# Order of the seven products, of the early operand splits and of the residual additions in the FFN down projection of a hybrid decoder layer

## The chip, the cores and the metric

The kernel runs on one core of one Trainium2 chip. The metric is the device time of one execution in microseconds, and the median of several executions is compared. The engines of a core are TensorE (PE, the matrix products), VectorE (DVE), ScalarE (ACT), GpSimd (POOL) and SyncE (SP, which here only issues DMAs). Each engine works through its own list of instructions in the order in which they were put there.

## The reference

One layer of a decoder for 1024 prompt tokens and 8 sample tokens (one new token for each of 8 sequences), width 1024, all in float32. The change lies in the last part, the feed-forward block:

```python
gate = h2 @ lp['w_ffn_gate']                    # (tokens, 2816)
up = h2 @ lp['w_ffn_up']                        # (tokens, 2816)
...
gc = _causal_dwconv(gate_ext, lp['ffn_conv_w'], L) + lp['ffn_conv_b']
x = x + gt2 * ((jax.nn.silu(gc) * up) @ lp['w_ffn_down'])
...
y_prompt = _rmsnorm(xp, final_norm_w)
```

Before it stand the input projection, a gated delta rule, a sliding-window attention and an output projection, which the change does not touch.

## The kernel before

**Precision.** A float32 operand is split into a high part (ACT, line 127, a copy into a rounded format) and a low part (DVE, line 128, the operand minus its high part). The helper `mm3` (lines 176 to 180) makes each product of two operands from three matmuls: high by high (L178), high by low (L179), low by high (L180).

**Seven products instead of eight.** The gate, up and down projections use a Strassen-Winograd scheme: both operands are cut into 2 x 2 blocks, and seven products of sums of blocks, numbered 1 to 7 in the down projection, replace eight products of blocks. Their results are added with signs to the four blocks of the output.

**Gate and up (`ffn_gate_up`, `pair_product`).** A loop goes over pairs `f` of 128-wide column blocks of the 2816, eleven pairs. For each pair the gate products are made, then the convolution and the activation on DVE and ACT (`conv`), then the up products. Both token halves `p` = 0 and 1 go through the seven products; `keep` copies an intermediate sum out of PSUM with ACT (L1563), and `up` evacuates a block with DVE (L1638 adds a kept copy, L1640 multiplies by the activated gate). When the four blocks of a token half are ready, `act_operands` has POOL make five sums of blocks (L1655), and writes these (L1658, one DMA from POOL's queue) and two plain blocks (L1657, from SP's queue) to `xd` in DRAM. `xd[i, g]` is the moving operand of kind `i` for the pair `g` = 0 to 10: kinds 0 to 4 are POOL's sums, 5 and 6 are plain blocks.

**Down (`ffn_down`).** A step is one product number `i` and one pair `g`; there are 7 x 11 = 77 steps, in the order of `chains`. `made[i]` says which kind of `xd` a product reads and which weight blocks: one block, or two, with their sum or difference. `fetch(s)` loads step `s`: the weight block (L1687), the second block if there is one (L1690) with the sum or difference on POOL (L1691), and the moving operand (L1692), all loads from SP's queue, into one of five raw buffers; then `split` writes the high and low parts into one of 13 rooms (`tags`), so that at most 13 steps are fetched ahead of PE. The rooms are those of the operands of the gate and up projections, and come free as the last up products have read them.

A step on PE has 24 matmuls: 4 column blocks `j` x 2 token halves `p` in eight PSUM banks, three matmuls each, summed over the eleven `g` of a product. Two products of one chain follow each other in the same banks without being cleared, so that the second adds to the first. After the last `g` of a product, `take` adds each bank to the residual `x1` (L1407, and L1411 with L1412 for the sample tokens): for products with one place in the output (4, 7, 6) directly from PSUM, for those with two places after an ACT copy (L1714) into one of eight buffers `copies`. All additions of a bank are issued at once, before the next product's matmuls:

```python
def take(ps, i, p, j):
    if len(home[i]) > 1:
        ...
        nc.scalar.copy(r, ps)
        ps = r
    for d, q, sign in home[i]:
        self.add_gated(2 * p + q, ps, j + 4 * d, 40, ...)
```

The last product, 6, is not in this loop: it runs bank by bank, with the final norm (`norm_rows`) of the rows that are ready between its banks.

**Order.** The functions issue instructions with priorities in the order of the program; a scheduler fixes each engine's list when the program is made, by times that it assumes. `tc.issue_after(x)` places the instructions of its block that run on the engine of `x` behind `x` in that list; it adds no wait at run time. So the splits of the first steps stand in DVE's and ACT's lists among the evacuations of the last up products, and the matmuls of the first steps fill PE between those products.

Of the kernel before, what the change touches and what calls it, by code (L numbers as in the profile page):

```python
# [22 lines left out]
KC = 8  # L23
# [39 lines left out]
class Step:  # L63
# [1479 lines left out]
    def pair_product(self, psum, w, pairs, evac, after={}):  # L1543

        nc = self.nc
        bank = lambda pl, tag, n: self.t(pl, [P, 512], tag, bufs=2)[:, :n]
        width = [QUARTERS[2 * p][1] for p in range(2)]
        x, v, y, r = {}, {}, {}, {}  # L1550

        def product(ps, p, i, first=True):

            (wh, wl), (xh, xl) = w[i], self.X[p][i]
            kw = {} if first else {"skip_group_check": True}
            with self.tc.issue_after(after[i].ins) if i in after else nullcontext():
                for k in range(4):
                    self.mm3(ps, wh[:, k, :], wl[:, k, :], xh[:, k, :], xl[:, k, :], first and k == 0, k == 3, **kw)

        def keep(p, i):  # L1560
            self.turn = (self.turn + 1) % KC
            r[p, i] = self.copies[:, self.turn, :width[p]]
            nc.scalar.copy(r[p, i], x[p])  # L1563

        for p in pairs:
            x[p] = bank(self.pmm, "mm", width[p])
            product(x[p], p, 0)
            keep(p, 0)
        for p in pairs:
            y[p] = bank(psum, "wy", width[p])  # L1570
            product(y[p], p, 1)
            evac(p, 0, 0, y[p], r[p, 0])
        for p in pairs:
            product(x[p], p, 2, False)
            keep(p, 1)
        for p in pairs:
            v[p] = bank(psum, "wv", width[p])
            product(v[p], p, 3)
        for p in pairs:
            product(x[p], p, 4, False)  # L1580
            keep(p, 2)
            evac(p, 1, 1, v[p], r[p, 2])
        for p in pairs:
            product(x[p], p, 5, False)
            evac(p, 1, 0, x[p], None)
        for p in pairs:
            product(v[p], p, 6, False)
            evac(p, 0, 1, v[p], r[p, 1])

    def ffn_gate_up(self, pool, pool2, psum, f, w, first):  # L1590

        nc, I = self.nc, self.I
        fcw = self.fcw
        z = [self.t(pool, [P, NT + 2], "fz", bufs=2) for _ in range(2)]
        for i in range(2):
            nc.gpsimd.memset(z[i][:, 0:2], 0.0)
        a = [self.act_tile(pool2) for _ in range(2)]
        done = {}

        def gate(p, i, q, ps, r):  # L1600
            lo, n = QUARTERS[2 * p + q]
            zq = z[i][:, 2 + lo:2 + lo + n]
            if r is None:
                nc.scalar.copy(zq, ps)
            else:
                nc.vector.tensor_tensor(zq, ps, r, op=ALU.add)
            done[p, i] = done.get((p, i), 0) + 1
            if done[p, i] == 2:
                conv(p, i)

        def conv(p, i):
            c, n = HALF[p]
            e = min(c + n, NP)
            zi, ai = z[i], a[i]
            col = lambda j: fcw[:, j, f + i:f + i + 1]
            nc.vector.tensor_scalar(ai[:, c:e], zi[:, 2 + c:2 + e], col(2), col(3), op0=ALU.mult, op1=ALU.add)
            for j in (0, 1):
                nc.vector.scalar_tensor_tensor(ai[:, c:e], zi[:, j + c:j + e], col(j), ai[:, c:e],  # L1618
                                               op0=ALU.mult, op1=ALU.add)
            if p:  # L1620
                nc.gpsimd.tensor_copy(self.fzl[:, f + i, :], zi[:, NP:NP + 10])
                nc.vector.scalar_tensor_tensor(ai[:, NP:], zi[:, 2 + NP:], col(2), self.fsp[:, f + i, :],
                                               op0=ALU.mult, op1=ALU.add)
            th = zi[:, c:c + n]
            nc.scalar.activation(th, ai[:, c:c + n], AF.Tanh)
            nc.vector.scalar_tensor_tensor(ai[:, c:c + n], th, 1.0, ai[:, c:c + n], op0=ALU.add, op1=ALU.mult)

        if first:
            ss, r = self.norm_at
            self.pair_product(psum, w, (0,), gate, {2: ss, 4: r})  # L1630
        self.pair_product(psum, w, (1,) if first else (0, 1), gate)
        w = self.pair_weights(pool, I["w_ffn_up"][0], f, nc.vector if first else None)

        def up(p, i, q, ps, r):
            lo, n = QUARTERS[2 * p + q]
            aq = a[i][:, lo:lo + n]
            if r is not None:
                nc.vector.tensor_tensor(r, ps, r, op=ALU.add)  # L1638
                ps = r
            nc.vector.tensor_tensor(aq, aq, ps, op=ALU.mult)  # L1640
            done[p, i] += 1
            if done[p, 0] == done[p, 1] == 4:
                self.act_operands(p, f // 2, a)

        self.pair_product(psum, w, (0, 1), up)
# [17 lines left out]
    def ffn_down(self, pool, psum):  # L1663
# [4 lines left out]
        made = {5: (2, (1, 1)), 3: (5, (0, 1), (1, 1), ALU.subtract), 4: (6, (1, 0), (0, 0), ALU.subtract),  # L1668
                7: (4, (1, 0), (1, 1), ALU.add), 1: (0, (0, 0), (1, 1), ALU.add), 2: (1, (0, 0)),
                6: (3, (0, 0), (0, 1), ALU.add)}  # L1670
        chains = ((4, 7), (3, 5), (1,), (2,), (6,))
        home = {3: ((0, 0, 1), (1, 1, 1)), 5: ((1, 0, 1), (0, 0, -1)), 4: ((0, 1, 1),), 7: ((0, 0, 1),),
                1: ((0, 0, 1), (1, 1, 1)), 2: ((0, 1, 1), (1, 1, -1)), 6: ((1, 1, 1),)}
        steps = [(i, g) for c in chains for i in c for g in range(G)]
        ready = {}
        less = []

        def fetch(s):
            i, g = steps[s]
            if s % 5 == 3:  # L1680
                ready["raw"] = self.t(self.bm, [P, KC, QW], "bmh0").rearrange("p k n -> p (k n)")
            raw = self.t(self.pw, [P, n + 512], "raw", bufs=3) if s % 5 < 3 else \
                ready["raw"][:, (s % 5 - 3) * 1040:(s % 5 - 3) * 1040 + n + 512]
            at, *src = made[i]
            src = [x if type(x) is not tuple else
                   I["w_ffn_down"][0][(2 * g + x[0]) * P:(2 * g + x[0] + 1) * P, 512 * x[1]:512 * x[1] + 512] for x in src]
            nc.sync.dma_start(raw[:, n:], src[0])  # L1687
            if len(src) > 1:
                other = self.t(self.pw, [P, 512], "ws", bufs=3)
                nc.sync.dma_start(other, src[1])  # L1690
                nc.gpsimd.tensor_tensor(raw[:, n:], raw[:, n:], other, op=src[2])  # L1691
            nc.sync.dma_start(raw[:, :n], self.xd[at, g])  # L1692
            room = self.room(tags[s % len(tags)], [P, KC * QW])
            hi, lo = room[:, :n + 512], room[:, n + 512:2 * (n + 512)]
            self.split(hi, lo, raw)
            ready[s] = hi, lo
            if s == 5:
                less.append(self.t(pool, [P, KC, 9], "less"))
                nc.gpsimd.tensor_scalar(less[0], self.mT[:, 40:48, :], -1.0, None, op0=ALU.mult)
                for j in (2, 3, 4):  # L1700
                    self.x1[j] = self.t(pool, [P, NT], f"x1_{j}")
                for j in range(2, 8):
                    nc.gpsimd.dma_start(self.x1[j], self.x1d[j])

        def step(s, ps, p, j, first, last, kw):
            hi, lo = ready[s]
            x, w = slice(256 * p, 256 * p + 256 + 4 * p), slice(n + j * P, n + j * P + P)
            self.mm3(ps, hi[:, w], lo[:, w], hi[:, x], lo[:, x], first, last, **kw)

        def take(ps, i, p, j):  # L1710
            if len(home[i]) > 1:
                self.turn = (self.turn + 1) % KC
                r = self.copies[:, self.turn, :256 + 4 * p]
                nc.scalar.copy(r, ps)  # L1714
                ps = r
            for d, q, sign in home[i]:
                self.add_gated(2 * p + q, ps, j + 4 * d, 40, self.mT[:, 40:48, :] if sign > 0 else less[0])

        banks = [(self.pmm, "mm", 2), (psum, "wv", 2), (psum, "wy", 2)] * 2 + [(self.pmf, "mm", 1), (psum, "nr", 1)]
        order = [(p, j) for j in range(4) for p in range(2)]  # L1720
# [1 line left out]
        for c in chains[:-1]:  # L1722
            ps = {(p, j): self.t(pl, [P, 512], tag, bufs=k)[:, :256 + 4 * p] for (p, j), (pl, tag, k) in zip(order, banks)}
            for i in c:
                for g in range(G):
                    while done < min(s + len(tags), len(steps)):
                        fetch(done)
                        done += 1
                    for p, j in order:
                        step(s, ps[p, j], p, j, g == 0 and i == c[0], g == G - 1, {"skip_group_check": True} if i != c[0] else {})  # L1730
                        if g == G - 1:
                            take(ps[p, j], i, p, j)
                    s += 1
        while done < len(steps):
            fetch(done)
            done += 1
# [3 lines left out]
        for k, (p, j) in enumerate((p, j) for p in (1, 0) for j in range(4)):  # L1740
            ps = self.t(self.pmf if k % 3 == 2 else self.pmm, [P, 512], "mm", bufs=1 if k % 3 == 2 else 2)[:, :256 + 4 * p]
            for g in range(G):
                step(s + g, ps, p, j, g == 0, g == G - 1, {})
            take(ps, 6, p, j)
            for c in chunks[k]:
                for _ in self.norm_rows(pool, psum, [c]):
                    pass
# [229 lines left out]
```

## Time and profile before

| | |
|---|---|
| time, median of 3 runs | 2173.14 us (2170.6 to 2176.24) |
| the profiled execution, its own time | 2178.02 us |
| its span from the first to the last instruction | 2176.3 us |
| mean granted TensorE clock | 0.974 |
| PE busy | 2084.8 us (96%) |
| DVE busy | 1394.8 us (64%) |
| ACT busy | 845.2 us (39%) |
| POOL busy | 517.6 us (24%) |

The times in the profile are microseconds from the start of the span. L1407 is line 1407 of the kernel. The last gate and up products run from about 1880, the down projection takes over between 1914 and 1939, and the last product runs from about 2123 on. A matmul stands with the time from its start to its modelled end, and starts about 0.12 us after the one before; a PE that is shown as idle had no matmul in that time at all. An entry such as `[2.00 <-ACT bml L1714]` says that the engine stood idle for 2.00 us before this instruction and which engine and line ended it.

### The profile page before, as it was taken

The page shows a single profiled execution, that of the slowest core. Times are in us where ns is not written, and L with a number is a line of the kernel's source. Part 1 is how long each engine was busy: PE and PEld are TensorE (multiplying, and loading weights), DVE is VectorE, ACT ScalarE, POOL GpSimd, SP SyncE. Part 2 cuts the span into 40 slices and gives each one's busy share as a digit, 9 for nine tenths or more (in the row PEclk, how much of TensorE's full clock was granted, in tenths as well). Part 3 has the DMA queues.
Part 4 walks back from the last instruction along what each step waited for, and adds up shares of the span by engine and source line. Part 5 has one row for each costly group of instructions (what it writes and reads, how often), then busy time and mean ns, then how long its engine had stood idle before and what let it go on. Part 6 is the DMA issues. An engine that isn't in the chain of part 4 may idle for free. (4 is left out here: it accounts for less than half of the span.)

```text
span 2176.3 us, 41336 instructions
## 1 busy us (share of the span) xinstructions
PE 2084.8 (96%) x16309; PEld 1960.8 (90%) x16309; DVE 1394.8 (64%) x2773; ACT 845.2 (39%) x2102; POOL 517.6 (24%) x589
## 2 busy tenths in 40 slices
PE   7998999999899999999999999999999999999998
PEld 4985887899898988998999999898999999989998
DVE  4656667374555756665323665478888788796885
ACT  4655445334234244344322032244343343333542
POOL 1000000021221110111110300003646556574330
PEclk8999998899999999999999999899999999999999
DMA  8256442151332321221317763511333332389862
GB/s 279 80 137 206 147 138 79 40 143 41 84 82 57 77 56 41 62 66 51 89 60 227 222 188 105 173 62 59 111 102 93 108 98 88 130 270 332 273 200 81
DMA packets 298980, 268.68 MB, mean 123 GB/s; under 512 B 60558, under 2 KB 246321, under 8 KB 298770
## 3 DMA queue, kind: packets, MB, share of 16 engines
q1 hardware_dynamic: 293586, 247.22, 37.5%
q0 software_dynamic: 4912, 18.29, 2.3%
q8 instruction: 128, 2.10, 0.4%
q14 instruction: 66, 0.54, 0.1%
q10 hardware_dynamic: 288, 0.52, 0.1%
HBM read 207.29 MB, written 61.07 MB: 123 GB/s over the span
## 5 line engine op out<-in xcount | busy, mean ns | idle before, releaser
L178 PE MATMUL mm<-b1h,wh 128*128 128x384 f32 (+1 forms) x1392 | 458.0, 330 | 4.5 <-ACT z L764 2.1
L180 PE MATMUL mm<-b1h,wl 128*128 128x384 f32 (+1 forms) x1392 | 453.0, 326 | 3.8 <-DVE wl L128 3.8
L179 PE MATMUL mm<-b1l,wh 128*128 128x384 f32 (+1 forms) x1392 | 450.6, 324 | 0.3 <-DVE b1l L128 0.3
L178 PEld LDWEIGHTS mm<-b1h,wh 128*128 128x128 f32 x1392 | 264.1, 190 | 14.8 <-issue 4.7
L180 PEld LDWEIGHTS mm<-b1h,wl 128*128 128x128 f32 x1392 | 263.9, 190 | 10.3 <-issue 5.5
L179 PEld LDWEIGHTS mm<-b1l,wh 128*128 128x128 f32 x1392 | 264.5, 190 | 3.6 <-issue 1.9
L127 ACT ACTIVATE wh<-raw 128x1024 fp32r<-128x1024 f32 x75 | 78.6, 1048 | 154.5 <-PE mm L179 77.6
L128 DVE TENSOR_TENSOR wl<-raw,wh 128x1024 fp32r<-128x1024 f32 x74 | 92.0, 1243 | 63.9 <-ACT wh L127 63.2
L178 PE MATMUL mm<-pk,w 128*128 128x260 f32 (+1 forms) x440 | 125.1, 285 | 3.0 <-ACT bml L1563 2.4
L179 PE MATMUL mm<-pk,w 128*128 128x260 f32 (+1 forms) x440 | 124.9, 284 | 0.8 <-DVE pk L128 0.8
L180 PE MATMUL mm<-pk,w 128*128 128x260 f32 (+1 forms) x440 | 124.7, 284 | 0.0
L178 PE MATMUL mm<-b2h,wh 128*128 128x384 f32 (+1 forms) x384 | 123.2, 322 | 0.4 <-ACT wh L127 0.4
L180 PE MATMUL mm<-b2h,wl 128*128 128x384 f32 (+1 forms) x384 | 122.0, 320 | 1.3 <-DVE wl L128 1.3
L179 PE MATMUL mm<-b2l,wh 128*128 128x384 f32 (+1 forms) x384 | 122.7, 320 | 0.0
L128 DVE TENSOR_TENSOR w<-ws,w 128x512 fp32r<-128x512 f32 x88 | 74.6, 849 | 36.5 <-ACT w L127 36.5
L178 PE MATMUL mm<-bmh,w 128*128 128x260 f32 (+1 forms) x320 | 92.0, 287 | 0.8 <-DVE fa L1640 0.7
L180 PE MATMUL mm<-bmh,w 128*128 128x260 f32 (+1 forms) x320 | 91.8, 287 | 0.0
L1563 ACT COPY bml<-mm 128x256 f32<-128x256 f32 (+1 forms) x132 | 49.1, 373 | 104.1 <-PE mm L180 97.6
L178 PEld LDWEIGHTS mm<-pk,w 128*128 128x128 f32 x440 | 83.3, 189 | 3.8 <-ACT bml L1563 3.0
L179 PEld LDWEIGHTS mm<-pk,w 128*128 128x128 f32 x440 | 83.4, 190 | 1.0 <-DVE pk L128 1.0
L180 PEld LDWEIGHTS mm<-pk,w 128*128 128x128 f32 x440 | 83.6, 190 | 0.0
L1618 DVE SCALAR_TENSOR_TENSOR fa<-fz,fcw,fa 128x512 f32<-128x512 f32 x88 | 75.0, 860 | 0.4
(639 smaller groups left out, 6076.6 us busy)
## 6 DMA issues: line engine op xcount, KB each, us to landing
raw<-in_w_in_dram SPq DMA_DIRECT2D x60, 512.0 KB
ws<-in_w_ffn_down_dram SPq DMA_DIRECT2D x55, 256.0 KB
raw<-xd SPq DMA_DIRECT2D x47, 258.0 KB
raw<-in_w_ffn_down_dram SPq DMA_DIRECT2D x47, 256.0 KB
raw<-in_w_ffn_gate_dram SPq DMA_DIRECT2D x22, 512.0 KB
raw<-in_w_ffn_up_dram SPq DMA_DIRECT2D x22, 512.0 KB
qst<-in_w_mod_dram SPq DMA_DIRECT2D x16, 512.0 KB
raw<-in_w_mod_dram SPq DMA_DIRECT2D x16, 512.0 KB
```

Source lines behind the costliest of these rows:

```text
L127: self.nc.scalar.activation(hi, x, AF.Copy)
L128: (eng or self.nc.vector).tensor_tensor(lo, x, hi.bitcast(F32), op=ALU.subtract)
L178: mm(ps, whi, xhi, start=first, stop=False, **kw)
L179: mm(ps, whi, xlo, start=False, stop=False, **kw)
L180: self.last_mm = mm(ps, wlo, xhi, start=False, stop=last, **kw).ins
L1563: nc.scalar.copy(r[p, i], x[p])
L1618: nc.vector.scalar_tensor_tensor(ai[:, c:e], zi[:, j + c:j + e], col(j), ai[:, c:e], op0=ALU.mult, op1=ALU.add)
```

## The change

- The order of the products becomes (5, 3), (4, 7), 1, 2, 6; before it was (4, 7), (3, 5), 1, 2, 6. Products 5 and 3 change places within their chain, so that the bank now holds first product 5 alone and then the sum of both; `home` is changed to match. Product 5 reads one plain weight block and kind 2 of `xd`; product 4, which came first, reads the difference of two weight blocks and the plain kind 6.
- The splits of steps 5 to 12 are placed behind the last `keep` copy on ACT and behind the last L1640 on DVE.
- The residual rows `x1_2` to `x1_7` are loaded from SP's queue, one after the fetch of each of the steps 18 to 23, instead of all six from POOL's queue after the fetch of step 5.
- `take` now copies every product of the loop out of PSUM with ACT and adds nothing. The additions go on two lists, the first place of each bank ahead of the second, and two of them are issued after each of the steps `g` = 2 to 9 of the next product. What is left after product 2 is issued before the last product. Product 6 is added directly from PSUM, as before.

```diff
-            nc.scalar.copy(r[p, i], x[p])
+            self.last_copy = nc.scalar.copy(r[p, i], x[p])
...
-            nc.vector.tensor_tensor(aq, aq, ps, op=ALU.mult)
+            self.last_up = nc.vector.tensor_tensor(aq, aq, ps, op=ALU.mult)
...
-        chains = ((4, 7), (3, 5), (1,), (2,), (6,))
-        home = {3: ((0, 0, 1), (1, 1, 1)), 5: ((1, 0, 1), (0, 0, -1)), 4: ((0, 1, 1),), 7: ((0, 0, 1),),
+        chains = ((5, 3), (4, 7), (1,), (2,), (6,))
+        home = {5: ((0, 0, -1), (1, 1, -1)), 3: ((1, 0, 1), (1, 1, 1)), 4: ((0, 1, 1),), 7: ((0, 0, 1),),
...
-        ready = {}
+        ready, waiting = {}, ([], [])
...
-            self.split(hi, lo, raw)
+            with ExitStack() as after:
+                if 5 <= s < len(tags):
+                    for ins in (self.last_up, self.last_copy):
+                        after.enter_context(self.tc.issue_after(ins.ins))
+                self.split(hi, lo, raw)
...
-                for j in range(2, 8):
-                    nc.gpsimd.dma_start(self.x1[j], self.x1d[j])
+            if 18 <= s < 24:
+                nc.sync.dma_start(self.x1[s - 16], self.x1d[s - 16])
...
+        def add(ps, p, j, d, q, sign):
+            self.add_gated(2 * p + q, ps, j + 4 * d, 40, self.mT[:, 40:48, :] if sign > 0 else less[0])
+
         def take(ps, i, p, j):
-            if len(home[i]) > 1:
-                self.turn = (self.turn + 1) % KC
-                r = self.copies[:, self.turn, :256 + 4 * p]
-                nc.scalar.copy(r, ps)
-                ps = r
-            for d, q, sign in home[i]:
-                self.add_gated(2 * p + q, ps, j + 4 * d, 40, self.mT[:, 40:48, :] if sign > 0 else less[0])
+            self.turn = (self.turn + 1) % KC
+            r = self.copies[:, self.turn, :256 + 4 * p]
+            nc.scalar.copy(r, ps)
+            for k, h in enumerate(home[i]):
+                waiting[k].append((r, p, j, *h))
...
+                    if g in range(2, 10):
+                        for _ in range(2):
+                            if waiting[0] or waiting[1]:
+                                add(*(waiting[0] or waiting[1]).pop(0))
                     s += 1
+        for x in waiting[0] + waiting[1]:
+            add(*x)
...
-            take(ps, 6, p, j)
+            add(ps, p, j, *home[6][0])
```

## The prediction

> **What bounds the kernel now.** I read the page first, then the busy time by stretches over the last 290 us, then the waits of each engine there, and last the timelines of DVE, POOL and PE at the places where PE stood still.
>
> The page:
>
> ```profile
> span 2176.3 us, 41336 instructions
> ...
> PE 2084.8 (96%) x16309; PEld 1960.8 (90%) x16309; DVE 1394.8 (64%) x2773; ACT 845.2 (39%) x2102; POOL 517.6 (24%) x589
> ```
>
> PE is busy 96% of the span, so a change that adds and removes no matmul can win only where PE idles or runs at a lower clock. The change touches the passage from the last up projection into the down projection, and the down projection. Busy time there, by stretches of unequal length (columns: length, then busy time and count per engine, granted clock, DMA share, GB/s):
>
> ```profile
> 1915.00:1925.00 10.00, 7.60 (x51) 7.39 (x50) 10.00 (x9) 4.66 (x7) 5.28 (x4) 0.83 0.80 247
> 1925.00:1940.00 15.00, 11.98 (x94) 11.16 (x93) 15.00 (x17) 3.20 (x3) 13.29 (x11) 1.00 0.81 250
> 1940.00:1955.00 15.00, 15.00 (x128) 15.00 (x127) 9.70 (x6) 5.25 (x6) 14.96 (x12) 1.00 0.93 312
> 1955.00:1975.00 20.00, 16.13 (x131) 15.50 (x131) 13.87 (x21) 5.28 (x5) 9.59 (x11) 1.00 1.02 377
> 1975.00:1980.00 5.00, 5.00 (x31) 5.00 (x31) 1.26 (x2) 2.01 (x2) 3.50 (x3) 0.66 1.05 395
> 1980.00:2060.00 80.00, 80.00 (x673) 80.00 (x671) 62.12 (x65) 35.80 (x41) 35.49 (x21) 1.00 0.83 273
> 2060.00:2065.00 5.00, 3.00 (x25) 2.80 (x24) 4.30 (x7) 4.78 (x11) 0.00 (x0) 1.00 0.97 333
> ```
>
> All that can be won stands here. First place, 1915 to 1940: 2.40 + 3.02 = 5.42 us idle; at clock 0.83, the 7.60 us of matmuls lose another 7.60 x 0.17 = 1.29 us; together 6.7. DVE is busy every microsecond of it. Second place, 1955 to 1980: 3.87 idle, and 5.00 x 0.34 = 1.70 at clock 0.66; together 5.6, with the DMA engines full. Third, at 2060: 2.00. The sum is 14.3 us, 0.66% of the span. Who held PE:
>
> ```profile
> PE mm L178 <- DVE x L1407: 2.8, 2, 2.3
> PE mm L178 <- ACT bml L1563: 2.4, 1, 2.4
> PE wv L178 <- DVE bml L1638: 2.4, 3, 1.5
> PE mm L178 <- ACT bml L1714: 2.0, 1, 2.0
> PE mm L178 <- DVE gtmp L1411: 1.1, 1, 1.1
> PE mm L178 <- DVE fa L1640: 0.7, 1, 0.7
> ```
>
> L1563, L1638 and L1640 evacuate the up products (first place, 5.5 us); L1407 and L1411 add product 4 of the down projection to the residual, and product 7 goes into the same banks (second); L1714 copies product 5 (third). In each case a PSUM bank is freed late, although the work that frees it is short.
>
> **The change, part by part.**
>
> *Splits 5 to 12 behind the last up evacuation.* The 1028-wide DVE subtractions (L128) that split a step's operand now stand between the up evacuations. Their busy time in one stretch, then the first of them and the last evacuation:
>
> ```profile
> 1921.50:1937.30 15.80, 8.47 (x5) 1.00 0.81 253
> ```
> ```profile
> 1922.18 1.22 DVE L128 TENSOR_TENSOR bml<-raw,bml 128x1028 fp32r<-128x1028 f32 x1
> ...
> 1937.42 1.50 DVE L1640 TENSOR_TENSOR fa<-fa,bml 128x256 f32<-128x256 f32 x2
> ```
>
> These are steps 5 to 9: 8.5 us ahead of the last evacuation, which ends at 1938.9. DVE is saturated, so the last evacuation moves up to about 1930.4. On ACT the same edge takes the split of step 5, which waited for POOL's weight sum, from in front of the copy L1563 (the 2.4 us). Behind the edge now wait eight ACT activations and eight DVE subtractions, 1.1 and 1.2 us each; PE has steps 0 to 4 meanwhile, 14 us of matmuls (a step is 24 matmuls, and 673 took 80 us: 2.85 us a step). Five raw buffers hold the operands of steps 5 to 9 until then, so SP's loads from step 10 on wait too, behind the same splits. Of the 6.7 us I keep 1.0 as lost (about two waits of the size of L1640's 0.7, halved because DVE has slack): a gain of 5.7, between 0 and 6.7.
>
> *Plain block first.* Steps 0 to 10 read one weight block instead of two: eleven loads of 256 KB on SP's queue and eleven POOL operations (L1691) leave the start, and come back when product 4 is made from step 22 on, at 80 us of which PE shows no idle time. The matmuls are the same in number and shape. The new cost is in step 10: its moving operand is a POOL sum that goes through DRAM, where before it was a plain block. That is the second rival.
>
> *Six residual loads.* Before, POOL issued them in one bunch as it reached step 5's place; now SP issues one behind each of steps 18 to 23:
>
> ```profile
> x<-x1d POOLq DMA_DIRECT2D x6, 516.0 KB, 9.9
> xd<-r POOLq DMA_DIRECT2D x2, 650.0 KB, 7.1
> xd<-r POOLq DMA_DIRECT2D x2, 640.0 KB, 5.4
> ```
>
> 6 x 516 KB at 395 GB/s is about 8 us of full DMA: the bunch fell into 1957 to 1980, held up the operands, and with them DVE's queue with the additions. Spread out, each adds 1.3 us to a step of 770 KB, which takes 1.95; 3.25 us a step against PE's 2.85 eats 0.4 x 6 = 2.4 us of a lead of up to 12 steps. A raw load queued on SP behind one of them comes 1.3 us later; nothing on PE waits for it as long as the lead is over one step.
>
> *Additions through copies, spread.* Every product but 6 is copied out of PSUM by ACT (16 copies more, 5.6 us of ACT by the copy's 0.35 below; ACT is 39% busy), and DVE adds two at a time during steps 2 to 9 of the next product. A bank is then free after a copy instead of after an addition. But an ACT copy stands in a queue with splits, as the third place shows:
>
> ```profile
> 2060.83 1.06 ACT L127 ACTIVATE bmh<-raw 128x1028 fp32r<-128x1028 f32 x1 [0.22 <-DMA raw<-xd]
> 2061.80 0.35 ACT L1714 COPY bml<-mm 128x256 f32<-128x256 f32 x1
> ```
>
> The copies waited behind a split of a later step whose data came late, and PE lost 2.00. Of the four products copied before, one had this. For the boundary from product 5 to 3, where the lead is shortest, I take a loss of 2.3 (that row and a third of a microsecond) instead of 5.6: a gain of 3.3, between 5.6 and a loss (first rival). For the five later boundaries together I take 1.0, half of what the third place shows, since DVE no longer does sixteen additions in one piece: a gain of 1.0. From below, the copies cost nothing; from above 2.0 at each of five boundaries, 10.0.
>
> What they cost on DVE:
>
> ```profile
> 1996.03 0.48 DVE L1407 SCALAR_TENSOR_TENSOR x<-mm,mT,x 128x260 f32<-128x260 f32 x1
> ...
> 2029.78 4.87 DVE L1407 SCALAR_TENSOR_TENSOR x<-bml,mT,x 128x256 f32<-128x256 f32 x4
> ```
>
> An addition from PSUM takes 0.48; four from copies in SBUF took 4.87, 1.2 each, while POOL summed weights. So the 16 additions of products 4 and 7 become up to 16 x 0.7 = 12 us dearer on DVE, over 22 steps or 63 us; that is slack in DVE. The Trainium skill (SBUF — State Buffer, section "SBUF: two separate sides") gives the cause: a VectorE operation with two SBUF inputs and a GpSimd operation that reads SBUF exclude each other for a whole instruction. The two rows agree; it speaks against this part of the change, and is the third rival.
>
> On the clock: after a wait of 2.4 and one of 2.3 us the granted clock fell to 0.83 and 0.66. The Trainium skill (TensorE: Matmul & The Clock Gate, section "What's actually happening") has the array throttled after an idle window of about 3.4 us; by that, neither wait would have cost clock, and the sum would lose 3.0 us, an estimate. The rows say otherwise and decide.
>
> **Sum.** 5.7 + 3.3 + 1.0 = 10.0 us. The profiled execution took 2178.0 us, 1.7 over its span; it would become 2168.0. The median of the three runs is 2173.14, 4.9 below it; by the same gain I predict **2163.1 us**. With all 14.3 won it is 2158.8. About 0.3%, 6.5 us, is what a measurement of this kernel can tell from no change.
>
> **The rivals.**
>
> *First: the stall stays at the boundary.* ACT's order is fixed when the program is made; if splits of steps whose data is late stand before the eight copies of product 5, the boundary costs 5.6 again (+3.3), and two more of the later ones cost 2.0 each (+4.0): 2170.4, no change to be told. For it: 2060. Against: three of four copied boundaries were clean, and from 1980 to 2060 PE had no gap with the same two-block loads. 12%.
>
> *Second, slower: step 10 waits for POOL's sum.*
>
> ```profile
> 1938.93:1949.84 10.91, 4.79 (x3) 1.00 0.86 276
> ```
> ```profile
> 1948.62 1.30 POOL L1691 TENSOR_TENSOR bmh<-bmh,ws 128x512 f32<-128x512 f32 x1
> 1949.84 0.87 POOL L1658 DMA_DIRECT2D xd<-r  x1
> ```
> ```profile
> 1902.83 3.92 DMA raw<-xd
> ...
> 1990.96 6.59 DMA raw<-xd
> ```
> ```profile
> 1956.62 0.28 PE L178 MATMUL mm<-pk 128*128 128x256 f32 x1
> ```
>
> The last sums leave at 1949.84, land 7.1 later, are read back in 3.9 to 6.6 and split in 2.3: 1963.1 to 1965.8. PE began step 10 at 1956.6 and, 5.7 earlier, wants it at 1950.9. If POOL is no faster, PE idles 12.2 to 14.9 us, 13.5 in the middle, with 1.7 of clock; the splits of later steps queue behind it on ACT and DVE, so that the next boundary loses its 3.3 too: 2163.1 + 18.5 = 2181.6. Slower. Against: POOL does the sums 11 us after the last evacuation while three weight sums (L1691, the stretch above) take 4.8 of them; without these, and with the evacuation at 1930.4, the issue is at 1930.4 + 6.1 = 1936.5, as 10.9 less 4.8 is 6.1. It decides from about 1935 to 1939 on (1950.9 less 2.3, 3.9 to 6.6, and 5.4 to 7.1): close, but a miss by 2 us costs 2, which the range holds. For the full price POOL must stay at 1949. 14%.
>
> *Third: DVE and POOL exclude each other in products 3 and 4.* A step there has a POOL sum of 1.30, a split of 1.22 and two additions of 0.5: 3.5 us if nothing overlaps, against 2.85 of PE: 0.65 x 8 = 5.2 us behind for each product, 10.4 for two. With a lead of one step, 2.85, PE starves 7.5: 2170.6. Against: between 1980 and 2060 both engines together were busy 62.12 + 35.49 = 97.6 us of 80, so a good part does overlap. 5%.
>
> *Fourth: it does not do what it says.* The edges fix an order but the evacuations stay late, held by the convolution's own DVE work: first place unchanged, 2168.8. Against: the five splits do stand between the evacuations. 5%.
>
> **How the numbers follow.** My forecast has 64%, with a range of its own from 2158.8 (all won) to 2168; 60 of the 64 lie below 2166.6. Within 0.3% fall the other 4 and rivals one, three and four (22): 26%. Slower is rival two: 14%. The range from 2158 to 2174 holds the forecast and rivals one, three and four with some 3 us beyond them, and leaves out rival two and some tails.
>
> **What would show it.** In the profile after: between the last gate evacuation and the last L1640, at most five 1028-wide DVE splits, the last L1640 near 1930 and PE's waits for L1563, L1638 and L1640 under 1.5 us in all; no L1691 for the first eleven steps; no PE wait for an addition at any boundary before product 6; PE's waits for the copies in take under 4 us. I am wrong if PE waits for a split of step 10 (rival two), if the copies hold PE for over 5 us (rival one), if PE waits for a split of a step of product 3 or 4 (three), or if DVE's evacuations still end after 1936 (four).

## The result and the profile after

The changed kernel takes 2160.84 us (median of four runs, 2160.1 to 2163.8), the kernel before 2174.22 on the same chip (2170.6 to 2176.24): ratio 0.9945, 95% interval 0.9929 to 0.996. In a second comparison on another chip it was 2163.97 against 2173.37: 0.9962 (0.9942 to 0.9981). It is faster by some 0.4 to 0.55%; the medians differ by 13.4 and 9.4 us.

First the page after, for the size of what PE still does not use:

```profile
span 2158.3 us, 41369 instructions
...
PE 2075.7 (96%) x16309; PEld 1957.4 (91%) x16309; DVE 1384.7 (64%) x2781; ACT 849.8 (39%) x2118; POOL 520.4 (24%) x583
```

The span is 18.0 us shorter. Not all of that is the change. To compare only the code that differs, I take one instruction that stands at the same place in every kernel, an ACT copy of the up projection, from here on **the marker**. Before and after:

```profile
1888.52 0.38 ACT L1563 COPY bml<-mm 128x260 f32<-128x260 f32 x1 [1.05 <-PE mm L180]
```
```profile
1880.73 0.38 ACT L1563 COPY bml<-mm 128x260 f32<-128x260 f32 x1 [1.05 <-PE mm L180]
```

Up to the marker PE runs the same 14105 matmuls, yet one profile is 7.8 us earlier: that is a difference between executions (in the thirteen profiles of this study the marker lies between 1880.7 and 1891.5). From the marker to the start of the last matmul of product 2, **the passage**, before takes 236.5 us and after 226.1, 10.4 less; the rest, **the tail** with product 6 and the outputs, 51.3 and 51.5. So the change is worth 10.4 us in one execution, and the profiles differ by 18.0.

The same times after, in which the code stands 7.8 us further on (columns: length, then busy time and count of PE, PEld, DVE, ACT, POOL, granted clock, DMA share, GB/s):

```profile
1915.00:1925.00 10.00, 10.00 (x86) 10.00 (x85) 7.72 (x6) 1.07 (x1) 6.94 (x6) 1.00 0.62 216
1925.00:1940.00 15.00, 15.00 (x128) 15.00 (x127) 7.73 (x6) 5.22 (x5) 7.30 (x6) 1.00 1.04 392
1940.00:1955.00 15.00, 15.00 (x129) 15.00 (x128) 13.15 (x27) 5.70 (x12) 5.76 (x4) 1.00 0.96 364
1955.00:1975.00 20.00, 20.00 (x169) 20.00 (x169) 15.18 (x10) 10.24 (x14) 13.58 (x9) 1.00 0.89 307
...
2005.00:2010.00 5.00, 1.74 (x14) 1.53 (x14) 2.69 (x3) 2.62 (x5) 3.59 (x3) 0.91 1.02 361
2010.00:2015.00 5.00, 5.00 (x24) 5.00 (x25) 5.00 (x6) 3.70 (x9) 3.37 (x3) 0.50 0.90 312
2015.00:2020.00 5.00, 5.00 (x41) 5.00 (x41) 5.00 (x10) 2.13 (x2) 3.21 (x3) 0.91 0.90 297
```

The first and the second place are gone: no idle PE and clock 1.00 from 1915 to 1975. One new place stands at 2005: 3.26 idle, and 0.16 + 2.50 + 0.45 = 3.1 us of lower clock. The view of the waits has one line left for PE:

```profile
PE mm L178 <- ACT bml L1720: 3.7, 2, 3.3
```

L1720 is the copy in `take` (L1714 before). At the boundary from product 4 to 7 the eight copies stand on ACT behind the splits of two later steps, which wait for POOL's weight sums:

```profile
2006.49 1.06 ACT L127 ACTIVATE bmh<-bmh 128x1028 fp32r<-128x1028 f32 x1 [2.44 <-POOL bmh L1691]
2008.44 1.06 ACT L127 ACTIVATE bmh<-bmh 128x1028 fp32r<-128x1028 f32 x1 [0.89 <-POOL bmh L1691]
2009.41 0.35 ACT L1720 COPY bml<-mm 128x256 f32<-128x256 f32 x1
```

### The profile page after: what moved, and what is told of

The parts are those of the page before. It is cut to its first block, busy times and chain, and to the rows that moved or that the text cites. A ratio compares the mean times of both kernels' runs of the same rounds, so it can differ in the third digit from the quotient of the medians.

```text
span 2158.3 us, 41369 instructions
## 1 busy us (share of the span) xinstructions
PE 2075.7 (96%) x16309; PEld 1957.4 (91%) x16309; DVE 1384.7 (64%) x2781; ACT 849.8 (39%) x2118; POOL 520.4 (24%) x583
## 5 line engine op out<-in xcount | busy, mean ns | idle before, releaser
L178 PEld LDWEIGHTS mm<-b2h,wh 128*128 128x128 f32 x384 | 72.7, 189 | 2.8 <-ACT wh L127 2.2
```

What stands on the lines that cost most here:

```text
L178: mm(ps, whi, xhi, start=first, stop=False, **kw)
```

## The experiments

Each kernel is compared with the kernel before on its own chip. Passage and tail are from one profile each, in us; "up end" is the end of the last L1640, counted from the marker.

| kernel | ratio (95%) | up end | passage | tail |
|---|---|---|---|---|
| before | 1 | 50.4 | 236.5 | 51.3 |
| changed | 0.9945 (0.9929 to 0.996) | 34.1 | 226.1 | 51.5 |
| changed_again | 0.9962 (0.9942 to 0.9981) | 34.1 | 226.2 | 51.7 |
| order_alone | 0.9996 (0.9977 to 1.0015) | 43.8 | 234.9 | 51.2 |
| edges_alone | 0.9994 (0.9978 to 1.0011) | 42.7 | 236.0 | 51.2 |
| no_edges | 0.9992 (0.9974 to 1.001) | 44.9 | 235.3 | 50.8 |
| adds_at_once | 0.997 (0.9952 to 0.9988) | 34.1 | 229.6 | 50.9 |
| x1_from_pool | 0.9982 (0.9968 to 0.9997) | 34.1 | 235.8 | 52.4 |
| spread_adds | 0.9988 (0.9969 to 1.0007) | 34.1 | 237.1 | 50.8 |
| copies_first | 0.9963 (0.9944 to 0.9981) | 34.1 | 219.9 | 58.3 |
| spread_copies | 1.0006 (0.9989 to 1.0023) | 34.1 | 231.4 | 57.1 |
| copies_first_mended | 0.9955 (0.994 to 0.997) | 34.1 | 219.9 | 55.8 |
| no_early_sums | one run, 2169.44 us | 44.1 | 229.4 | 51.2 |

**The plain block first, alone.** The kernel before with only the new order of products.

```diff
-        chains = ((4, 7), (3, 5), (1,), (2,), (6,))
+        chains = ((5, 3), (4, 7), (1,), (2,), (6,))
...  (and the signs in home for products 3 and 5)
```

> The kernel before with only the new order of the products (5, 3), (4, 7), 1, 2, 6; splits not held back, six residual loads in one bunch from POOL's queue, additions at once. Theory (POOL's weight sums were as much of the trouble at the up evacuations as the splits were): with no L1691 in the first eleven steps DVE's instructions there are no longer stretched, the last L1640 comes 10 to 13 us earlier than before, PE idles under 2 us before the first down product ends, against 5.4; the bunch of loads then costs up to 5 us at the first boundary: 2164 to 2170 us. Rival (the five splits among the evacuations were the trouble): PE still idles 4 us or more there, 2170 to 2174 us.

The up evacuations end 6.6 us earlier and PE waits for none of them. But PE stands still at step 10, for a split, and its passage is only 1.6 us shorter:

```profile
PE mm L178 <- ACT pk L127: 8.7, 1, 8.7
PE mm L178 <- DVE x L1407: 3.0, 2, 2.6
```
```profile
L1658 POOL DMA_DIRECT2D xd<-r x2: 874/874/874, 1932.6 to 1934.9; - x2
```

POOL's sums, the operand of step 10, are sent to DRAM at 1934.9 (last start in that view), 52.2 behind the marker; in the changed kernel 38.9 behind it. The gain of this part becomes a new wait, the second rival's. My expectation missed: 6.6 us in place of 10 to 13, and 2174.92 us in place of 2164 to 2170.

**The edges alone.** The kernel before with `last_copy`, `last_up` and the `issue_after` round the split of steps 5 to 12, as in the change.

> The kernel before with only the splits of steps 5 to 12 placed behind the last up copy and the last L1640; the old order, loads and additions. Theory: the evacuations come about 8 us earlier, POOL's weight sums of steps 0 to 4 still stretch them; PE idles about 2 us there instead of 5.4; the second place, product 4's additions behind late splits, stays at 5 to 6 us or grows, since the operands come later: 2168 to 2174 us. Rival (the splits were the whole of the first place): 6 us gained, and more at the second: 2165 to 2168 us.

The last evacuation ends 7.7 us earlier, close to the 8.5 us of splits that the prediction took out of DVE's list. It is not enough:

```profile
PE mm L178 <- ACT bml L1718: 4.4, 2, 3.3
PE wv L178 <- DVE bml L1638: 2.5, 1, 2.5
PE mm L178 <- ACT bml L1563: 1.6, 1, 1.6
```

The first place keeps 4.1 us of waits of its 5.5, where I had expected about 2, and the copies of two products, behind the splits on ACT, take 4.4. The passage is 0.5 us shorter, and the time does not differ from that of before.

**The change without the edges.**

```diff
-            with ExitStack() as after:
-                if 5 <= s < len(tags):
-                    for ins in (self.last_up, self.last_copy):
-                        after.enter_context(self.tc.issue_after(ins.ins))
-                self.split(hi, lo, raw)
+            self.split(hi, lo, raw)
```

> The changed kernel without the placing of the splits of steps 5 to 12. Theory: with plain blocks these splits wait neither for POOL nor run long, so they cost DVE 5 x 1.2 = 6 us among the evacuations, which PE's own filling with early steps covers for the most part: 1 to 4 us slower than the changed kernel, 2162 to 2165 us. Rival (the placing makes the gain): the first place returns with 5 us or more: 2166 to 2170 us.

My expectation of 2162 to 2165 us fell: 2174.39, ratio 0.9992. No evacuation holds PE, but step 10 does, worse than in order_alone:

```profile
PE mm L178 <- ACT pk L127: 9.7, 1, 9.7
```
```profile
1942.52 0.87 POOL L1658 DMA_DIRECT2D xd<-r  x1
...
1944.76 0.87 POOL L1658 DMA_DIRECT2D xd<-r  x1
```
```profile
1959.98 1.04 ACT L127 ACTIVATE pk<-raw 128x1028 fp32r<-128x1028 f32 x1
```

The sums leave 53.3 us behind the marker, 1.1 later than in order_alone, and PE's pause at step 10 is 9.94 us instead of 9.01. In these two profiles that is about one for one: the pause ends with the chain of evacuation, sum, DRAM, split. One link more stands in it. The sums land 5.2 and 7.8 us after their issue, by 1952.6 at the latest, but a load from `xd` leaves SP only at 1955.04, the last one before this split, behind a weight load (L1690, 1954.32) that waited for POOL; in order_alone the like load leaves at 1945.06 and the split starts as it lands.

The edges earn their place not by the evacuations alone but by bringing POOL's sums in time for the plain block's last step. With them the sums leave 14.4 us earlier behind the marker: 10.8 us are the last evacuation (44.9 to 34.1), and the other 3.6 are about what two weight sums of later steps take (L1691, 2.27 and 1.40 us), which POOL makes in no_edges ahead of the last operand sums' issue, and in the changed kernel behind it.

**Does POOL's summing stretch the evacuations?** The kernel before, in which POOL leaves out its sum of two weight blocks in the first eleven steps (both are still loaded).

```diff
+                if s >= 11:
-                nc.gpsimd.tensor_tensor(raw[:, n:], raw[:, n:], other, op=src[2])
+                    nc.gpsimd.tensor_tensor(raw[:, n:], raw[:, n:], other, op=src[2])
```

> The kernel before, with POOL's sum of two weight blocks left out in the first eleven down steps (both blocks are still loaded, the second is not added): does POOL's summing stretch DVE's operations on the last up evacuations? Theory: it does; without the sums the operation that multiplies two taps (L1618) takes 0.75 us in place of 1.24, and the last up evacuation ends some 44 us behind the marker, like in the kernel that had only the new order of products, in place of 50.4. Rival: the new order brought it forward because its first splits are issued at other places; then without the sums it stays at 49 to 50.4 us.

It does. The last eight operations L1618, each of which adds one tap of the convolution (count, then busy us and mean ns), in before, after and this kernel:

```profile
L1618 DVE SCALAR_TENSOR_TENSOR fa<-fz,fcw,fa 128x512 f32<-128x512 f32 x8 | 9.9, 1243 | 0.0
```
```profile
L1618 DVE SCALAR_TENSOR_TENSOR fa<-fz,fcw,fa 128x512 f32<-128x512 f32 x8 | 6.0, 751 | 0.0
```
```profile
L1618 DVE SCALAR_TENSOR_TENSOR fa<-fz,fcw,fa 128x512 f32<-128x512 f32 x8 | 6.0, 747 | 0.0
```

In before, four of the eight took 1.65 to 1.80 us, each beside a weight sum of POOL, and the other four 0.74. The last evacuation ends 44.1 us behind the marker, expected 44. So the order of products alone brings it forward by 6.6 us, the edges alone by 7.7, and the changed kernel, which has both, by 16.3.

The passage of this kernel is 229.4 us, 7.1 less than before. PE's waits for the evacuations fall from 5.5 to 0.2 us; what is left is one wait of 6.5 us for an addition, at the boundary from product 4 to 7. The kernel leaves work out and was run once, so it shows a cause and not a time that can be had.

**The additions as before.** The changed kernel, but products 4 and 7 are added straight from PSUM and every addition is made in `take`.

```diff
-            self.turn = (self.turn + 1) % KC
-            r = self.copies[:, self.turn, :256 + 4 * p]
-            nc.scalar.copy(r, ps)
-            for k, h in enumerate(home[i]):
-                waiting[k].append((r, p, j, *h))
+            if len(home[i]) > 1:
+                ...                    (the copy, as in before)
+            for h in home[i]:
+                add(ps, p, j, *h)
```

The residual loads are issued one step earlier each, so that they are in time for the earlier additions.

> The changed kernel with the additions as before: at once after each product, products 4 and 7 directly from PSUM, 5, 3, 1 and 2 through copies; the six residual loads start one step earlier, since they are needed earlier. Theory (the additions are a burst on DVE in both, because the list of DVE takes them as soon as they are ready; the copies free the banks): boundaries of 5 and 3 the same, PE waits for DVE's additions after product 4 behind splits that come late, 3 to 6 us as in the changed kernel: 2159 to 2165 us. Rival (the spreading and the copies carry the gain): second place returns, 2166 to 2170 us.

One wait is left, at the same boundary, from product 4 to 7, and it is longer; the passage is 3.5 us longer than in the changed kernel:

```profile
PE mm L178 <- DVE x L1407: 7.1, 1, 7.1
```
```profile
2013.58 1.94 DVE L128 TENSOR_TENSOR bmh<-bmh,bmh 128x1028 fp32r<-128x1028 f32 x1 [2.53 <-ACT bmh L127]
2015.44 0.47 DVE L1407 SCALAR_TENSOR_TENSOR x<-mm,mT,x 128x256 f32<-128x256 f32 x1
```

Here the additions that free the banks stand on DVE behind the splits of later steps, as the copies stand on ACT in the changed kernel. The copies do not end that wait, they shorten it. The time, 2167.85 us, lies outside the 2159 to 2165 that I expected and within the rival's 2166 to 2170.

**The residual loads from POOL's queue.**

```diff
-            if 18 <= s < 24:
-                nc.sync.dma_start(self.x1[s - 16], self.x1d[s - 16])
+                for j in range(2, 8):
+                    nc.gpsimd.dma_start(self.x1[j], self.x1d[j])      (at s == 5)
```

> The changed kernel, but the six loads of the residual rows are issued from POOL in one bunch at the sixth step, as in the kernel before, instead of one for each of steps 18 to 23 from SP. Theory: the six loads of 512 KB or more each then run beside the loads of the first eleven steps and beside POOL's sums; what they delay is the splits of steps 10 to 15, whose margin in the changed kernel was about 2 us, so PE waits 2 to 6 us near 59 us behind the marker (where two other kernels showed a wait of 9 to 10 us for the split of step 10). Ratio 0.9955 to 0.998. Rival: the bunch is issued behind POOL's last sum and its bytes are carried before they are missed: passage 226 us within 1, ratio 0.9945.

```profile
PE mm L178 <- ACT bml L1720: 10.8, 3, 6.7
PE mm L178 <- ACT pk L127: 0.9, 1, 0.9
PE mm L179 <- DVE pk L128: 0.9, 1, 0.9
```
```profile
1941.26 1.06 ACT L127 ACTIVATE pk<-raw 128x1028 fp32r<-128x1028 f32 x1 [11.51 <-DMA raw<-xd]
```

Step 10's split starts 59.8 us behind the marker (55.3 in the changed kernel, row below), after ACT stood idle for 11.5 us until its operand landed, and PE waits 1.8 us there, a little under the 2 to 6 expected. At three later boundaries 10.8 us of waits for copies follow, with the copies behind late splits on ACT as in the changed kernel; that the lost lead makes these splits late is argued, not tested by itself. This part of the change is worth 9.7 us of passage, though on SP the six loads go out within 8 us of each other (1930 to 1938), not one a step of PE: the loads run ahead of the steps.

```profile
1936.07 1.05 ACT L127 ACTIVATE pk<-raw 128x1028 fp32r<-128x1028 f32 x1
```

**Additions really spread.** In the changed kernel DVE takes the additions of a product as soon as its copies are there, those of product 5 in one run of 9 us (first, one of the middle, last row):

```profile
1943.00 1.67 DVE L1407 SCALAR_TENSOR_TENSOR x<-bml,less,x 128x256 f32<-128x256 f32 x4
...
1948.69 1.27 DVE L1412 TENSOR_TENSOR x<-x,gtmp 128x8 f32<-128x8 f32 x1
...
1952.05 0.28 DVE L1412 TENSOR_TENSOR x<-x,gtmp 128x8 f32<-128x8 f32 x2
```

This kernel holds each pair back until the split eight steps ahead has been made:

```diff
-                                add(*(waiting[0] or waiting[1]).pop(0))
+                                with self.tc.issue_after(lows[s + 8].ins):
+                                    add(*(waiting[0] or waiting[1]).pop(0))
```

> The changed kernel, but each pair of additions may only stand on DVE behind the subtraction of the split eight steps ahead, so that they are truly spread, one pair to a split. Theory: the one stall left in the changed kernel (PE waits 3.26 us for a copy on ACT at the boundary from product 4 to product 7, and some 3 us go to the lower clock behind it) comes from the additions, which DVE takes in bursts (1943 to 1952 and 1975 to 1988) and which hold up the splits, their raw buffers and the loads. Spread, the copies find ACT free: the passage from the marker to the last product of chain (2) falls from 226.1 to 220 to 222 us, the time to about 2155 on the changed kernel's 2160.8 (ratio to the kernel before 0.991 to 0.993). Rival: the rate of POOL and the two-block loads sets the lead of the splits, not the additions; then the stall of 3 to 7 us stays at that boundary and the ratio stays at 0.9945 within its interval.

My theory fell: the passage is 11 us longer than in the changed kernel. The eight copy buffers are free only when both additions of a copy are done, and now the next product's copies wait for that:

```profile
1978.36 0.37 ACT L1721 COPY bml<-mm 128x256 f32<-128x256 f32 x1 [5.26 <-DVE x L1407]
```

PE's waits for these copies come to 10.9 us. The bursts of additions are early, and that keeps the copy buffers free; that they are not what held the boundary either, the next kernel shows.

**Copies ahead of the far splits.** The loads stay as they are, but at a product's end the splits more than five steps into the next product are put behind the eight copies on ACT (`fetch` is cut into `load` and `part`; `advance(loads, splits)` runs them up to a step).

```diff
-                    while done < min(s + len(tags), len(steps)):
-                        fetch(done)
-                        done += 1
+                    most = min(s + len(tags), len(steps))
+                    advance(most, min(most, s - g + G + 5))
...
+                    if g == G - 1:
+                        with self.tc.issue_after(self.last_take.ins):
+                            advance(most, most)
```

> The changed kernel, but at each product's end the splits of more than five steps ahead may only stand on ACT behind the eight copies. Theory: the wait at the boundary from product 4 to 7 is nothing but order on ACT (the copies stand behind the splits of steps 38 and 39, which wait for POOL and a load): with the copies ahead, the 3.26 us and the lower clock behind them go, the passage falls to 220 to 222 us, ratio 0.991 to 0.993. Rival: the splits of steps 38 and 39 are late whatever the order; PE then waits for one of them some steps later for the same 3 to 7 us, and the ratio stays near 0.9945; a shorter lead behind each boundary could add waits of 1 to 3 us each, ratio up to 0.998.

The passage is 219.9 us with no wait of PE at all, as the theory had it. At the same boundary the copies now come before the two splits:

```profile
2011.56 0.37 ACT L1735 COPY bml<-mm 128x256 f32<-128x256 f32 x1 [0.21 <-PE mm L180]
...
2014.35 1.07 ACT L127 ACTIVATE bmh<-bmh 128x1028 fp32r<-128x1028 f32 x1
2015.70 1.07 ACT L127 ACTIVATE bmh<-bmh 128x1028 fp32r<-128x1028 f32 x1 [0.29 <-POOL bmh L1693]
```

So the stall of 3.3 us, with its clock, was order on ACT. But the ratio is 0.9963, not the 0.991 to 0.993 expected: the tail became 6.8 us longer and took the gain back. Product 6 runs each bank through all eleven steps and needs all its splits at once, and here six of them stood behind the last copies. PE's longest waits in the tail:

```profile
PE mm L178 <- ACT pk L127: 1.7, 1, 1.7
PE mm L178 <- DVE gtmp L1411: 1.5, 1, 1.5
```
```profile
2116.27 1.21 DVE L128 TENSOR_TENSOR pk<-raw,pk 128x1028 fp32r<-128x1028 f32 x1
```
```profile
2123.90 1.06 ACT L127 ACTIVATE pk<-raw 128x1028 fp32r<-128x1028 f32 x1 [10.32 <-POOL raw L1693]
```

ACT had made five of the six high halves by 2113.6, but the low halves stood on DVE behind the additions of product 2, and the first came at 2116.27 (first row). As it ended, at 2117.5, the weight load of the sixth step left SP; its sum on POOL and its split (second row) followed, and PE's 1.7 us are the wait for that split. So the order on ACT and the additions on DVE worked together here.

**Both together.** The two edits above in one kernel:

```diff
+                                with self.tc.issue_after(lows[min(s + 8, at[1] - 1)].ins):
```

> The changed kernel with both of these: additions one pair to a split, and the copies ahead of the splits of more than five steps ahead. Theory: no PE wait above 1 us from the first down step to the last of chain (2), passage 219.5 to 221 us, ratio 0.991 to 0.992; it is no better than the better of the two alone by more than 2 us if both cure the same stall. Rival: the loads' rate bounds the lead, and a stall of 3 to 7 us appears wherever the lead runs out; ratio about 0.9945.

Ratio 1.0006, passage 231.4: the spread additions undo what the copies win. The theory missed here too, by the cause that spread_adds showed: from 1965 to the end of the passage the copies stand still for DVE's additions for 13.3 us.

**Copies first, but not before the last product.**

```diff
-                    advance(most, min(most, s - g + G + 5))
+                    advance(most, min(most, s - g + G + (5 if i != chains[-2][-1] else G)))
```

> The kernel with the copies ahead of the far splits (passage 219.9 us with no wait of PE, but a tail of 58.3 us in place of 51.5), with the order kept free at the last boundary, the one before the final product: there every split of the final product is needed within some 4 us, because one pair runs through all its eleven steps at once. Theory: the passage stays at 219.9 us and the tail falls back to 51.5 us, so the profile has the span of the changed kernel less 6 us in this part, the time is 2154 to 2156 us on the changed kernel's 2160.8 and the ratio to it 0.997. Rival: the 7 us in the tail come from additions that DVE had put off and has to make up at the end, not from the five splits behind the copies; then the tail stays near 58 us and the ratio to the changed kernel near 1.000.

The passage stays at 219.9 us; the tail goes from 58.3 to 55.8, not to 51.5. PE waits in it for one low half:

```profile
PE mm L179 <- DVE pk L128: 2.2, 1, 2.2
```
```profile
2105.60 1.59 DVE L1407 SCALAR_TENSOR_TENSOR x<-bml,mT,x 128x256 f32<-128x256 f32 x1
...
2111.33 1.22 DVE L128 TENSOR_TENSOR pk<-bmh,pk 128x1028 fp32r<-128x1028 f32 x1
```

```profile
2106.94 1.07 ACT L127 ACTIVATE pk<-bmh 128x1028 fp32r<-128x1028 f32 x1 [1.72 <-POOL bmh L1693]
```

ACT had made the high half by 2108.01; DVE's additions of product 2, from 2105.6 on, stand before the low half at 2111.33. So both theories of this run hold in part: of the 6.8 us, 2.5 went with the order at the last boundary, and by these rows the 2.2 of the wait go to the additions. Most of the rest is the lower clock behind that wait: the 361 matmuls of the tail keep PE busy for 44.2 us here and for 42.6 in the changed kernel. A kernel that puts the additions behind the low half was not run. By the profiles this kernel is 2.1 us shorter than the changed one from the marker on (275.7 against 277.9 in the same set); by the times, 2162.61 against 2163.97, the two cannot be told apart.

**The changed kernel again**, beside it:

> The changed kernel itself, beside the one with the copies first, so that the two are compared on one chip. Theory: the ratio to the kernel before is 0.9945 to 0.9955, the profile shows the same passage of 226 us with its one wait of 3.3 us at the boundary from product 4 to 7 within 1 us. Rival: the 10 us gained in the passage were one execution's luck; then the passage is 229 us or more.

Its passage is 226.2 us, within 0.1 of the first profile, though the marker lies 2.4 us later, and its one long wait stands at the same boundary with 3.98 us instead of 3.26. So on the changed kernel's side the 10.4 us are no luck of one execution; the kernel before was profiled once. The ratio, 0.9962, is a little above the 0.9945 to 0.9955 expected.

## Why the prediction was right, point by point

**The size.** 2163.1 us were forecast, in a range from 2158 to 2174, and 2160.84 and 2163.97 measured. Of a gain of 10.0 us the passage shows 10.4, and both comparisons of times (13.4 and 9.4 us) lie round it. That this comes so close is partly luck. In the prediction's own measure, idle time and clock by windows, the three steps brought 6.7 for the first place, 5.6 for the boundary from 5 to 3, and 4.8 less than nothing for the later boundaries (2.0 lost before, 6.8 after): 7.5 in all, against 5.7 + 3.3 + 1.0. The errors went both ways, and the passage holds some 3 us that this measure does not count.

**First place: gain 5.7 forecast, 6.7 found.** Nothing is left of it; the 1.0 kept as lost was not lost. But the reason given covers about half of the shift. The last evacuation was to move from 1938.9 to 1930.4, 41.9 us behind the marker of before; it came at 34.1:

```profile
1914.41 0.45 DVE L1640 TENSOR_TENSOR fa<-fa,bml 128x260 f32<-128x260 f32 x1
```

The forecast of 8.5 us for the splits was good (7.7 in edges_alone). The missing term is POOL: its weight sums stretched DVE's operations (1243 ns for a tap, 747 without the sums), and with the plain block first they go (6.6 us in order_alone, 6.3 in no_early_sums). The prediction had the row for it, four additions in 4.87 us, but used the effect only against the change, in the third rival. The Trainium skill (SBUF — State Buffer, section "SBUF: two separate sides") says that a VectorE operation with two SBUF inputs and a GpSimd operation that reads SBUF exclude each other for a whole instruction; no_early_sums agrees with it. For PE the split between the two parts is plainer still: with the new order alone no wait for an evacuation is left, and with the edges alone 4.1 us of the 5.5 stay, not 1.0. What the edges are needed for is the second rival, below.

**Plain block first: at no cost, except rival two.** No L1691 in the first eleven steps, as forecast; their return made no idle time that the order on ACT does not remove, since copies_first has the same sums and no wait in the passage.

**Six residual loads: no term of their own.** The prediction put them in the second place's total. Put back, they cost 9.7 us of passage, nearly all that the whole change wins. The parts do not add: order and edges alone win 1.6 and 0.5, the change without the edges 1.2, without the new place of the loads 0.7. Leaving out either of the last two gives nearly the whole gain back.

**Boundary 5 to 3: a loss of 2.3 forecast, 0 found.** The five later boundaries: 1.0 forecast, 6.8 found: 3.26 + 3.1 at 4 to 7 and 0.4 before product 6. This is the step that failed: the first rival's mechanism, at a later boundary than it named, and the estimate "half of what the third place shows" had no clock in it. The forecast of under 4 us of waits for copies held with 3.7 in the first profile and missed with 4.8 in the second. In the prediction's own measure the loss falls from 14.3 to 6.8 us, 7.5 less; by the starts of the matmuls the excess over one every 0.119 us falls from 16.8 to 6.4. The starts agree with the passage: a matmul's row is 0.28 us long though the next starts 0.12 later, so each of the nine pauses of before cost 0.16 more than the idle time shows, 1.4 us of the 2.5 between 14.3 and 16.8. The other 1.1 have no place yet.

**Additions "spread over steps 2 to 9".** They are written so and not done so: DVE's list takes them in bursts. The copies and the deferral are worth 3.5 us of passage (adds_at_once), forecast 3.3 + 1.0.

**The second rival** did not come, by a margin that can be read: the sums leave at

```profile
1918.78 1.75 POOL L1658 DMA_DIRECT2D xd<-r  x2
```

the second of the two 38.9 us behind the marker, against 48.0 forecast and a turning point of 46.5 to 50.5. At 52.2 and 53.3, in order_alone and no_edges, PE lost 9.0 and 9.9 us, so by one for one the turning point lies near 43, and the price for the 61.3 of before would be 18 us, an estimate from these two, not 12.2 to 14.9: PE wants step 10 59.7 us behind the marker, 2.7 earlier than the forecast had it. The rival was nearer than the prediction made it, and POOL's sums came 9 us earlier than it had them. It did tie the sums to the evacuation that the edges move; that without the edges the new order wins next to nothing was not in it.

**The third rival:** the stretching is there (the 8-wide L1412 at 1948.69 took 1.27 us and ended with the sum below, a row of the chain that ended last; the wider L1407 from 1943.00 on took 0.42 each with no sum beside them), but PE waits for no split of products 3 and 4.

```profile
1947.96 2.00 POOL bmh L1691
```

**The fourth:** the change does what it says, but for the spreading.

## What to carry to other kernels

When a stall is an instruction that frees a PSUM bank behind work that is not yet needed, look at the order on that one engine before its load: eight copies put ahead of two late splits took 6.2 us out of the passage, while spreading the work before it made things worse. Hold back only what is not needed at once: with the same order in front of a product that wants all its operands the tail grew by 6.8 us, of which the order at that boundary accounts for 2.5. And measure the changed stretch from a common instruction, since the time of the code ahead of it, which had not changed, varied by about as much as the whole gain from one execution to the next.

## What was not expected of the hardware

Some waits of 2.3 us and more lowered the granted clock, and others as long did not. It fell to 0.83 and 0.66 before, behind waits of 2.4 and 2.3 us, and to 0.91, 0.50 and 0.91 in three slices of 5 us after the 3.26 us here, as dear as the wait itself; behind the 3.98 us of changed_again the same count gives 1.4 us. The wait of 2.00 at 2060 before left it at 1.00, and so did one of 2.63 us at 2022 in order_alone and one of 2.71 us at 1981 in x1_from_pool:

```profile
2020.00:2025.00 5.00, 2.58 (x22) 2.61 (x23) 4.92 (x10) 2.18 (x3) 2.99 (x2) 1.00 1.02 344
```
```profile
1980.00:1985.00 5.00, 4.18 (x35) 4.19 (x36) 4.46 (x6) 4.61 (x11) 3.10 (x3) 1.00 0.98 342
```

So the length of a single wait does not settle whether clock is lost, and what does stays open. The Trainium skill (TensorE: Matmul & The Clock Gate, section "What's actually happening") names an idle window of about 3.4 us; the traces have the drop behind some shorter waits, and not behind all.
